# A two-layer encoder: the last layer's second product without a stored S2, with a second pool for weights, and with S1 made in two halves

## Chip, cores and metric

The kernel runs on one core of one Trainium2 chip. The metric is the device time of one execution in microseconds (us), the median of several runs.

## What is computed

The reference is an encoder of two layers over 1024 tokens of 1024 channels, in float32. Each layer has a mixer, a cross attention to 256 memory rows, and a feed-forward part; each of the three is normalised, added to the residual and stored.

```python
for i in range(DEPTH):                      # DEPTH = 2
    h = rms_norm(x, norm_mix[i, 0])
    if i % 2 == 0: mix = pool_and_conv_mixer(h)      # first layer
    else:          mix = s5_and_hyena_mixer(h)       # last layer
    x = x + rms_norm(mix, norm_mix[i, 1])
    h = rms_norm(x, norm_xattn[i, 0])
    m = rms_norm(mem, norm_mem[i])
    x = x + rms_norm(memory_cross_attention(h, m, ...), norm_xattn[i, 1])
    h = rms_norm(x, norm_mlp[i, 0])
    x = x + rms_norm(squared_relu_mlp(h, mlp_w1[i], mlp_w2[i]), norm_mlp[i, 1])

def squared_relu_mlp(xn, w1, w2):           # w1 1024 x 4096, w2 4096 x 1024
    h = jax.nn.relu(xn @ w1)
    return (h * h) @ w2
```

## The kernel before

**Numbers in two parts.** A matrix product is made of three matmuls (`mm3`, L263): each operand is held as a high and a low part in the fp32r format, and high*high, high*low and low*high are summed in PSUM. The two parts come from `split` (L258): a copy on ScalarE (L256) and a subtraction on VectorE (all tensor-tensor operations have L238). A weight block (128 rows by 1024) is therefore loaded as float32 into a buffer, split into a weight tile of twice the size, and used.

**Pools.** SBUF tiles come from pools of a fixed number of buffers: "h" (`hslot`, 9 buffers of 8 KB per partition), "a" (`slot`, 8), "w" (weight tiles, 4), "r" (`raw`, loaded blocks of 512 KB, 2), "t" (`tmp`, 3), "n" (`ntmp`, 3). A pool gives out its buffers in the order in which the program asks for them. In the profile a tile's name starts with its pool's letter, and a label of the stage follows (`wdn`, `adn`, `rdn`: "w", "a" and "r" buffers of the second product).

**Order.** A framework plans the order of the instructions of each engine when the program is built: it goes by due order, and what stands under `tc.high_priority()` goes first, as soon as its buffers are free. Weight loads, splits and the work on PSUM results are marked like that. On an engine the instructions then run strictly in that order; a DMA is issued from the queue of the engine named (`nc.sync`: SyncE, `nc.scalar`: ScalarE, `nc.gpsimd`: GpSimd), and waits there for its buffers.

**The feed-forward parts.** `mlp_up` makes the hidden values by a scheme with seven products in place of eight (sums of blocks in advance). Its loop over p = 0..15 uses `prep(p)` (L736), which loads two weight blocks, forms four sums of them and splits them; `prep(p + 1)` is called ahead of the products of p. In the first layer the loop runs interleaved with the preparation of the S5 mixer (`s5_prep`, L1402, small VectorE operations; it holds one "h" buffer from its start). In the last layer the hidden values are stored in seven forms in a DRAM array `HO`.

**The last layer's second product** is `mlp_q` (L918). It has seven products, i = 0..6, each over eight blocks of the hidden dimension; a step takes two blocks, so there are 28 steps j of 48 matmuls of 512 columns. `a11, a12, a21, a22` are the quarters of w2. Product 2 needs `S2 = S1 - a11`, product 3 `a11 - a21`, product 5 `S1 = a21 + a22`, product 6 `a12 - S2`. `load(j + 1)` is called ahead of step j: it loads two tiles of `HO` through "t" into "h" buffers (`hload`) and two weight blocks (`wload`). Where a block is a difference of two, both are loaded into one "a" buffer, subtracted there and split into a "w" buffer; in product 2 the difference is also stored to the DRAM array `SB` by a DMA on ScalarE's queue (L956), and product 6 loads it again. Four more "a" buffers come to hold the results (U, c11, c12, c22). After product 4 the first half of the tokens gets its residual; the last two steps are run together, token half by token half, and the second half's residual ends the kernel.

**S1** is made by DMAs alone, in `down_sums` (L905): one small DMA that ties its start to a tile `after`, and for each of eight blocks a copy of a21 into the DRAM array `SA` and a DMA that adds a22 to it, all on GpSimd's queue. It is called between the last layer's mixer and its attention. The attention (`attention`, L631) makes the scores (`scores`, L589, with blocks of G as weights), their softmax and the product with VW (`proj_out`, L422, which also does the residual, loading x on GpSimd's queue, L398). The mixer ends in the same `proj_out`, after a gate (`s5_gate`, L1673).

Of the kernel before, what the change touches and what calls it, by code (L numbers as in the profile page):

```python
# [18 lines left out]
P = 128  # L19
# [9 lines left out]
WINDOWS = (2, 4, 8, 16)  # L29
PI = math.pi  # L30
# [155 lines left out]
class Net:  # L186
# [444 lines left out]
    def attention(self, l, GV, H, xsrc, xdst):  # L631
        G, VW = GV
        PT = self.scores(G, H)
        return self.proj_out(VW, lambda hf, k: PT[hf][k], xsrc, self.gain("xattn", l, 1), xdst, self.gain("mlp", l, 0), quads=True)

# [43 lines left out]
    def mlp_up(self, l, B, HID, HO=None):  # L679
# [91 lines left out]
        nxt = prep(0)  # L771
        for p in range(16):
            c, S1, S2, S3, S4, A22 = nxt
            if p < 15:
                nxt = prep(p + 1)
            if HO is not None:
                to = HO[:, p // 2, :, (p % 2) * 512:(p % 2 + 1) * 512].rearrange("i p t -> p i t")
                with self.tc.high_priority():
                    e = self.hslot([4, 512])
                    nc.gpsimd.dma_start(e[:, 0], to[:, 0])  # L780
# [124 lines left out]
    def down_sums(self, l, after):  # L905

        nc = self.nc
        w2 = self.i["mlp_w2q"][l - 1]
        self.S1[l] = S1 = self.dram([8, P, 1024], f"SA{l}")

        nc.gpsimd.dma_start(S1[:, 0, 0:1].rearrange("n c -> c n"), after.bitcast(F32)[0:1, 0:8])
        for n in range(9):
            if n < 8:
                nc.gpsimd.dma_start(S1[n], w2[n, 1, 0])
            if n > 0:
                nc.gpsimd.dma_start(S1[n - 1], w2[n - 1, 1, 1], accum_op=ALU.add, max_dma_last_dim=4096)

    def mlp_q(self, l, B, xsrc, xdst, gnext, res):  # L918
# [10 lines left out]
        S1, S2 = self.S1[l], self.dram([8, P, 1024], f"SB{l}")  # L929
# [3 lines left out]
        s1, s2 = lambda c: S1[c], lambda c: S2[c]  # L933
        prods = [(True, (a11,), 0), (False, (a12,), 1), (True, (s1, a11), 4), (False, (a11, a21), 5),
                 (False, (a22,), 2), (True, (s1,), 3), (False, (a12, s2), 6)]
        steps = [(i, c) for i in range(7) for c in range(0, 8, 2)]

        def hload(i, c):
            t = self.tmp([2, 512])
            nc.gpsimd.dma_start(t[:].rearrange("p a t -> p (a t)"), HO[prods[i][2], c])  # L940
            h = self.hslot([2, 2, 512], F32R)
            self.split(h[:, 0], h[:, 1], t[:])
            return h

        def wload(i, c):
            src = prods[i][1]
            if len(src) == 1:
                return self.wblk(src[0](c))
            r = self.slot([2, 1024])
            for k in range(2):  # L950
                nc.sync.dma_start(r[:, k], src[k](c))
            self.sub(r[:, 0], r[:, 0], r[:, 1])
            w = self.wp.tile([P, 2, 1024], F32R, tag="w", name=self.nm("w"))
            self.split(w[:, 0], w[:, 1], r[:, 0])
            if i == 2:
                nc.scalar.dma_start(S2[c], r[:, 0])  # L956
            return w

        def load(j, h=None):
            i, c = steps[j]  # L960
            with self.tc.high_priority():
                h = h or [hload(i, c + q) for q in range(2)]
                return [wload(i, c + q) for q in range(2)], h
# [9 lines left out]
        for i, _ in enumerate(self.mlp_up(l, B, None, HO)):  # L973
            yield
            if i == 22:
                h = [hload(0, q) for q in range(2)]
# [842 lines left out]
    def mix1(self, H, xsrc, xdst, stop=None):  # L1819
# [70 lines left out]
        rhs = lambda hf, k: tuple(Y[k][:, s, hf * 512:(hf + 1) * 512] for s in range(2))  # L1890
        return self.proj_out(self.i["od_w_out"][0], rhs, xsrc, self.gain("mix", 1, 1), xdst, self.gain("xattn", 1, 0), (4, 5, 6, 7, 0, 1, 2, 3), late=2)

    def run(self, stop=None, first=0):
# [50 lines left out]
        self.down_sums(1, H[1][7][0])  # L1944
# [24 lines left out]
```

## Time and profile before

| what | value |
|---|---|
| median of 3 runs | 2913.18 us (2903.13 to 2919.44) |
| the profiled execution | 2913.07 us, of which the span is 2911.3 us |
| TensorE (PE) busy | 2767.3 us, 95% of the span |
| TensorE weight loads (PEld) busy | 2311.9 us, 79% (beside the matmuls) |
| VectorE (DVE) busy | 2038.3 us, 70% |
| ScalarE (ACT) busy | 1088.0 us, 37% |
| GpSimd (POOL) busy | 260.3 us, 9% |
| moved by DMA | 515.93 MB, mean 177 GB/s |

The page shows one execution; the last columns of a timeline row are the operation, the tiles (output<-inputs), and in brackets the idle time before it with what ended that. Busy shares are means over stages of very different kinds, so a stage is read by itself: the first layer's `mlp_up` lies at about 711 to 1048 us, the last layer's mixer ends at about 2050 (its output product starts near 1925), its scores lie at about 2048 to 2165, the attention's output product follows until about 2250, `mlp_up` until 2576, and the second product until the end. TensorE's matmuls are pipelined, so a busy TensorE need not be at its full pace; the number of matmuls in a stretch tells the pace.

### The profile page before, as it was taken

How to read it: one execution, taken by the hardware profiler on the slowest of the kernel's cores; microseconds unless marked ns; L12 is line 12 of the kernel's file. 1: busy time of each engine (PE TensorE's matmuls, PEld its weight loads, DVE VectorE, ACT ScalarE, POOL GpSimd, SP SyncE). 2: the span in 40 equal slices, each digit the busy share in tenths (PEclk: the TensorE clock that was granted, in tenths of full speed). 3: DMA queues.
4: the chain of work that ended last, by engine and by line, in shares of the span. 5: the costliest groups of instructions: out<-in, count | busy, mean ns of one | idle time of the engine just before them, and what ended most of it. 6: DMA issues, size and time to landing. Idle time of an engine off the chain costs nothing. (4 is left out here: it accounts for less than half of the span.)

```text
span 2911.3 us, 35912 instructions
## 1 busy us (share of the span) xinstructions
PE 2767.3 (95%) x13832; PEld 2311.9 (79%) x13832; DVE 2038.3 (70%) x3375; ACT 1088.0 (37%) x1304; POOL 260.3 (9%) x468
## 2 busy tenths in 40 slices
PE   8998999999999999999999988889999999998997
PEld 7877888988777877788878877768988778777886
DVE  6676546847899756695877788955846878755676
ACT  4344324444543442222343211233433544453341
POOL 0000000000211111010000000000010222210010
PEclk9999999999999999999999999999999999999999
DMA  5582214324644464342347688744363766688672
GB/s 177 209 286 102 69 44 138 102 87 145 230 170 145 143 199 137 121 152 80 120 161 234 218 264 272 276 160 129 114 185 119 241 227 224 216 282 319 225 262 104
DMA packets 177011, 515.93 MB, mean 177 GB/s; under 512 B 18820, under 2 KB 64008, under 8 KB 169672
## 3 DMA queue, kind: packets, MB, share of 16 engines
q1 hardware_dynamic: 87160, 244.99, 25.6%
q0 software_dynamic: 57872, 238.06, 23.7%
q10 hardware_dynamic: 31808, 30.60, 3.1%
q8 instruction: 108, 1.77, 0.2%
q14 instruction: 63, 0.52, 0.1%
HBM read 380.40 MB, written 141.56 MB: 179 GB/s over the span
## 5 line engine op out<-in xcount | busy, mean ns | idle before, releaser
L265 PE MATMUL mdn<-hdn,wdn 128*128 128x512 f32 (+1 forms) x752 | 287.4, 382 | 7.8 <-ACT wdn L256 7.5
L266 PE MATMUL mdn<-hdn,wdn 128*128 128x512 f32 (+1 forms) x752 | 287.4, 382 | 0.0
L267 PE MATMUL mdn<-hdn,wdn 128*128 128x512 f32 (+1 forms) x752 | 287.2, 382 | 0.0
L265 PEld LDWEIGHTS mdn<-hdn,wdn 128*128 128x128 f32 x752 | 142.0, 189 | 36.3 <-ACT wdn L256 8.3
L265 PE MATMUL mup<-apre,wup 128*128 128x512 f32 x384 | 153.4, 399 | 13.6 <-DVE hup L238 13.5
L266 PEld LDWEIGHTS mdn<-hdn,wdn 128*128 128x128 f32 x752 | 142.0, 189 | 27.5 <-issue 0.6
L267 PEld LDWEIGHTS mdn<-hdn,wdn 128*128 128x128 f32 x752 | 142.0, 189 | 27.4 <-DVE wdn L238 1.0
L267 PE MATMUL mup<-apre,wup 128*128 128x512 f32 x384 | 151.7, 395 | 0.1
L266 PE MATMUL mup<-apre,wup 128*128 128x512 f32 x384 | 151.8, 395 | 0.0
L256 ACT ACTIVATE wup<-rup 128x1024 fp32r<-128x1024 f32 x69 | 73.0, 1060 | 194.8 <-PE mup L267 183.0
L265 PE MATMUL msc<-wsc,hpre 128*128 128x256 f32 x448 | 128.3, 286 | 1.6 <-ACT hpre L256 1.6
L266 PE MATMUL msc<-wsc,hpre 128*128 128x256 f32 x448 | 129.5, 289 | 0.0
L267 PE MATMUL msc<-wsc,hpre 128*128 128x256 f32 x448 | 128.5, 288 | 0.4 <-DVE hpre L238 0.4
L238 DVE TENSOR_TENSOR hup<-hup,mup 128x512 f32<-128x512 f32 x128 | 87.5, 684 | 57.5 <-PE mup L267 56.4
L238 DVE TENSOR_TENSOR hdn<-tdn,hdn 128x1024 fp32r<-128x1024 f32 x74 | 90.4, 1222 | 52.3 <-ACT hdn L256 52.0
L266 PE MATMUL mmx<-hpre,wmx 128*128 128x512 f32 x320 | 124.7, 390 | 0.0
L256 ACT ACTIVATE hdn<-tdn 128x1024 fp32r<-128x1024 f32 x74 | 78.2, 1056 | 124.6 <-PE mdn L267 100.3
L265 PE MATMUL mmx<-hpre,wmx 128*128 128x512 f32 x320 | 124.7, 390 | 0.0
L267 PE MATMUL mmx<-hpre,wmx 128*128 128x512 f32 x320 | 124.5, 389 | 0.0
L238 DVE TENSOR_TENSOR wout<-rout,wout 128x1024 fp32r<-128x1024 f32 x48 | 58.7, 1222 | 87.6 <-ACT wout L256 87.6
L256 ACT ACTIVATE wdn<-rdn 128x1024 fp32r<-128x1024 f32 x53 | 55.9, 1056 | 140.7 <-PE mdn L267 129.4
L265 PE MATMUL mue<-hpre,wue 128*128 128x512 f32 x256 | 101.1, 395 | 1.1 <-ACT tue L256 1.1
(520 smaller groups left out, 7848.3 us busy)
## 6 DMA issues: line engine op xcount, KB each, us to landing
tdn<-HO POOLq DMA_DIRECT2D x50, 512.0 KB, 4.9
nres<-x POOLq DMA_DIRECT2D x44, 512.0 KB, 5.0
rup<-mlp_w SPq DMA_DIRECT2D x33, 512.0 KB, 3.9
x<-hout POOLq DMA_DIRECT2D x32, 512.0 KB, 5.1
rue<-mlp_w SPq DMA_DIRECT2D x32, 512.0 KB, 3.8
hup<-mlp_w SPq DMA_DIRECT2D x32, 512.0 KB, 4.4
wmx<-fwd POOLq DMA_DIRECT2D x16, 1024.0 KB, 7.3
HO<-hup POOLq DMA_DIRECT2D x16, 1024.0 KB, 6.0
```

Source lines behind the costliest of these rows:

```text
L238: self.nc.vector.tensor_tensor(out=out, in0=a, in1=b, op=op)
L256: self.nc.scalar.activation(out, a, AF.Copy)
L265: t.matmul(out, l[0], r[0], start=start, stop=False, **kw)
L266: t.matmul(out, l[0], r[1], start=False, stop=False, **kw)
L267: t.matmul(out, l[1], r[0], start=False, stop=stop, **kw)
```

## The change

It has four parts. (1) Product 2's difference is no longer stored: `SB` and its eight stores are gone, and product 6 makes its weights from three loaded operands, `a12 + S1 - a11`. (2) Loaded operands go elsewhere: where there are two or three, the first two go into one "h" buffer and a third into an "r" buffer; the split weights of every odd step go into an "a" buffer, those of even steps into a "w" buffer as before; within a load all fetches come first, then the weights' splits, then those of `HO`. (3) `down_sums` makes four blocks of S1 per call: the first four are tied to the gate's last output and called ahead of the mixer's `proj_out`, the other four are tied to the last head of the second token half and called between the scores and the attention's `proj_out`. (4) In the first layer's `mlp_up`, `prep(p)` is called at the start of iteration p; in the last layer nothing changes there.

```diff
--- before.py
+++ after.py
@@ -27,6 +27,7 @@
 MAGIC = 12582912.0
 RSQ = float(0x5F3759DF)
 WINDOWS = (2, 4, 8, 16)
+QUADS = (1,)
 PI = math.pi
 
 
@@ -631,6 +632,8 @@
     def attention(self, l, GV, H, xsrc, xdst):
         G, VW = GV
         PT = self.scores(G, H)
+        if l in QUADS:
+            self.down_sums(l, 1, PT[1][0][0])
         return self.proj_out(VW, lambda hf, k: PT[hf][k], xsrc, self.gain("xattn", l, 1), xdst, self.gain("mlp", l, 0), quads=True)
 
 
@@ -768,12 +771,11 @@
                 nc.gpsimd.dma_start(c[:, 0], P1[p])
             return c, S1, S2, S3, S4, (w[:, 0], w[:, 1])
 
-        nxt = prep(0)
+        nxt = prep(0) if HO is not None else None
         for p in range(16):
-            c, S1, S2, S3, S4, A22 = nxt
-            if p < 15:
-                nxt = prep(p + 1)
+            c, S1, S2, S3, S4, A22 = nxt or prep(p)
             if HO is not None:
+                nxt = prep(p + 1) if p < 15 else None
                 to = HO[:, p // 2, :, (p % 2) * 512:(p % 2 + 1) * 512].rearrange("i p t -> p i t")
                 with self.tc.high_priority():
                     e = self.hslot([4, 512])
@@ -902,17 +904,20 @@
             with self.tc.high_priority(offset=300 if hf == 0 else 0):
                 res.append(finish(hf, acc))
 
-    def down_sums(self, l, after):
+    def down_sums(self, l, part, after):
 
         nc = self.nc
         w2 = self.i["mlp_w2q"][l - 1]
-        self.S1[l] = S1 = self.dram([8, P, 1024], f"SA{l}")
-
-        nc.gpsimd.dma_start(S1[:, 0, 0:1].rearrange("n c -> c n"), after.bitcast(F32)[0:1, 0:8])
-        for n in range(9):
-            if n < 8:
+        if part == 0:
+            self.S1[l] = self.dram([8, P, 1024], f"SA{l}")
+        S1 = self.S1[l]
+        lo = 4 * part
+
+        nc.gpsimd.dma_start(S1[lo:lo + 4, 0, 0:1].rearrange("n c -> c n"), after.bitcast(F32)[0:1, 0:4])
+        for n in range(lo, lo + 5):
+            if n < lo + 4:
                 nc.gpsimd.dma_start(S1[n], w2[n, 1, 0])
-            if n > 0:
+            if n > lo:
                 nc.gpsimd.dma_start(S1[n - 1], w2[n - 1, 1, 1], accum_op=ALU.add, max_dma_last_dim=4096)
 
     def mlp_q(self, l, B, xsrc, xdst, gnext, res):
@@ -926,41 +931,52 @@
         nc = self.nc
         w2 = self.i["mlp_w2q"][l - 1]
         HO = self.dram([7, 8, P, 1024], f"HO{l}")
-        S1, S2 = self.S1[l], self.dram([8, P, 1024], f"SB{l}")
+        S1 = self.S1[l]
 
 
         a11, a12, a21, a22 = [lambda c, m=m, q=q: w2[c, m, q] for m in range(2) for q in range(2)]
-        s1, s2 = lambda c: S1[c], lambda c: S2[c]
+        s1 = lambda c: S1[c]
         prods = [(True, (a11,), 0), (False, (a12,), 1), (True, (s1, a11), 4), (False, (a11, a21), 5),
-                 (False, (a22,), 2), (True, (s1,), 3), (False, (a12, s2), 6)]
+                 (False, (a22,), 2), (True, (s1,), 3), (False, (a12, s1, a11), 6)]
         steps = [(i, c) for i in range(7) for c in range(0, 8, 2)]
 
-        def hload(i, c):
+        def hfetch(i, c):
             t = self.tmp([2, 512])
             nc.gpsimd.dma_start(t[:].rearrange("p a t -> p (a t)"), HO[prods[i][2], c])
+            return t
+
+        def hparts(t):
             h = self.hslot([2, 2, 512], F32R)
             self.split(h[:, 0], h[:, 1], t[:])
             return h
 
-        def wload(i, c):
+        def wfetch(i, c):
             src = prods[i][1]
-            if len(src) == 1:
-                return self.wblk(src[0](c))
-            r = self.slot([2, 1024])
-            for k in range(2):
-                nc.sync.dma_start(r[:, k], src[k](c))
-            self.sub(r[:, 0], r[:, 0], r[:, 1])
-            w = self.wp.tile([P, 2, 1024], F32R, tag="w", name=self.nm("w"))
-            self.split(w[:, 0], w[:, 1], r[:, 0])
-            if i == 2:
-                nc.scalar.dma_start(S2[c], r[:, 0])
+            rs = []
+            if len(src) > 1:
+                r = self.hslot([2, 1024])
+                rs += [r[:, 0], r[:, 1]]
+            if len(src) != 2:
+                rs.append(self.raw.tile([P, 1024], F32, tag="r", name=self.nm("r"))[:])
+            for r, x in zip(rs, src):
+                nc.sync.dma_start(r, x(c))
+            return rs
+
+        def wparts(rs, odd):
+            for x, op in zip(rs[1:], (ALU.subtract, ALU.add)):
+                self.tt(rs[0], rs[0], x, op)
+            w = self.slot([2, 1024], F32R) if odd else self.wp.tile([P, 2, 1024], F32R, tag="w", name=self.nm("w"))
+            self.split(w[:, 0], w[:, 1], rs[0])
             return w
 
-        def load(j, h=None):
+        def load(j, hs=None):
             i, c = steps[j]
+            cs = range(c, c + 2)
             with self.tc.high_priority():
-                h = h or [hload(i, c + q) for q in range(2)]
-                return [wload(i, c + q) for q in range(2)], h
+                rs = [wfetch(i, c) for c in cs]
+                ts = hs or [hfetch(i, c) for c in cs]
+                ws = [wparts(r, j % 2) for r in rs]
+                return ws, hs or [hparts(t) for t in ts]
 
         def run(t, ws, hs, i, first, stop, tok=slice(0, 512)):
             for q, (w, h) in enumerate(zip(ws, hs)):
@@ -973,7 +989,7 @@
         for i, _ in enumerate(self.mlp_up(l, B, None, HO)):
             yield
             if i == 22:
-                h = [hload(0, q) for q in range(2)]
+                h = [hparts(hfetch(0, q)) for q in range(2)]
         nxt = load(0, h)
         acc = None
         for j, (i, c) in enumerate(steps):
@@ -1888,6 +1904,7 @@
         merge((self.s5_gate(*gg, Y), 8), (gv, 3))
         Y += hy
         rhs = lambda hf, k: tuple(Y[k][:, s, hf * 512:(hf + 1) * 512] for s in range(2))
+        self.down_sums(1, 0, Y[3][:, 0])
         return self.proj_out(self.i["od_w_out"][0], rhs, xsrc, self.gain("mix", 1, 1), xdst, self.gain("xattn", 1, 0), (4, 5, 6, 7, 0, 1, 2, 3), late=2)
 
     def run(self, stop=None, first=0):
@@ -1941,7 +1958,6 @@
         if stop == "mix1":
             return
         x2 = dst("x5", "att1")
-        self.down_sums(1, H[1][7][0])
         H = self.attention(1, self.GV[1], H, x1, x2)
         if stop == "att1":
             return
```

## Rows read from the trace of the kernel before

**Rows 1.** The page: busy us (share of the span) and instructions.

```profile
PE 2767.3 (95%) x13832; PEld 2311.9 (79%) x13832; DVE 2038.3 (70%) x3375; ACT 1088.0 (37%) x1304; POOL 260.3 (9%) x468
```

**Rows 2.** Table of stages: window, length, engines' busy us (instructions), clock, DMA share, GB/s.

```profile
2650.00:2675.00 25.00, 25.00 (x112) 20.71 (x111) 13.43 (x12) 9.95 (x10) 2.29 (x5) 1.00 0.96 348
2675.00:2700.00 25.00, 17.42 (x66) 13.39 (x65) 13.01 (x11) 6.97 (x7) 1.59 (x3) 0.80 0.88 324
```

**Rows 3.** Waits of TensorE, 2600 to 2860: us in total, times, longest us.

```profile
PE mdn L265 <- ACT wdn L256: 7.5, 1, 7.5
PE mdn L265 <- DVE adn L238: 0.3, 1, 0.3
```

**Rows 4.** Timelines of SP, DVE, ACT, PE, 2650 to 2695 [idle before].

```profile
2653.24 0.32 SPq L951 DMA_DIRECT2D adn<-SA  x1
2666.02 24.35 SPq L951 DMA_DIRECT2D adn<-mlp_w2q  x10
...
2677.03 1.23 DVE L238 TENSOR_TENSOR adn<-adn 128x1024 f32<-128x1024 f32 x1 [2.06 <-DMA adn<-mlp_w2q]
...
2678.29 3.04 ACTq L956 DMA_DIRECT2D SB<-adn  x2
2683.34 1.06 ACT L256 ACTIVATE wdn<-adn 128x1024 fp32r<-128x1024 f32 x1 [5.34 <-DMA SB<-adn]
...
2684.45 0.79 PE L265 MATMUL mdn<-hdn,wdn 128*128 128x512 f32 x1 [7.54 <-ACT wdn L256]
```

**Rows 5.** DMA, 2640 to 2700: 40 slices, total, issues (us to landing).

```profile
GB/s 339 235 161 371 382 388 401 423 415 415 423 404 407 388 169 303 322 279 164 360 385 279 391 418 415 426 412 339 314 246 350 134 270 401 347 350 320 82 322 396
DMA packets 5486, 20.02 MB, mean 334 GB/s; under 512 B 607, under 2 KB 607, under 8 KB 5482
...
adn<-mlp_w2q SPq DMA_DIRECT2D x15, 512.0 KB, 7.8
...
SB<-adn ACTq DMA_DIRECT2D x6, 512.0 KB, 5.0
```

**Rows 6.** Table of stages and chain (start, us, what) in the scores.

```profile
2110.00:2120.00 10.00, 10.00 (x85) 10.00 (x84) 3.51 (x4) 2.12 (x2) 3.57 (x5) 1.00 0.98 260
...
2130.00:2140.00 10.00, 6.58 (x45) 6.39 (x44) 4.29 (x10) 4.08 (x11) 2.12 (x3) 0.84 1.02 297
...
2120.01 11.27 DMA rsc<-G
...
2136.55 1.67 PE xsc L626 x8
```

**Rows 7.** Timeline of GpSimd's queue, 1900 to 2310.

```profile
1999.34 0.53 POOL L398 DMA_DIRECT2D nres<-x  x1 [78.75 <-DVE nout L238]
...
2105.42 0.53 POOL L911 DMA_DIRECT2D SA<-hpre  x1 [34.83 <-ACT hpre L256]
...
2143.03 0.83 POOL L916 DMA_DIRECT2D SA<-mlp_w2q  x1 [4.10 <-DMA SA<-mlp_w2q]
2206.24 0.58 POOL L398 DMA_DIRECT2D nres<-x  x1 [62.38 <-issue]
```

**Rows 8.** Table of stages; DVE near 1956; DMA issues 2165 to 2200.

```profile
1950.00:1975.00 25.00, 25.00 (x112) 20.69 (x111) 6.96 (x8) 8.29 (x11) 0.00 (x0) 1.00 0.18 61
...
1955.94 0.69 DVE L238 TENSOR_TENSOR amx<-tmx,amx 128x512 fp32r<-128x512 f32 x1 [0.70 <-ACT amx L256]
...
rout<-VW SPq DMA_DIRECT2D x4, 512.0 KB, 3.1
```

**Rows 9.** Table of stages, at the start of product 5.

```profile
2800.00:2825.00 25.00, 24.85 (x113) 20.09 (x112) 22.95 (x36) 10.52 (x11) 5.29 (x10) 1.00 0.69 239
```

**Rows 10.** DMA, 2800 to 2870: total.

```profile
DMA packets 4042, 15.80 MB, mean 226 GB/s; under 512 B 452, under 2 KB 452, under 8 KB 3782
```

**Rows 11.** Waits of TensorE, 700 to 1060 and then 2254 to 2580.

```profile
PE mup L265 <- DVE hup L238: 10.6, 7, 2.5
...
PE mup L265 <- DVE hup L238: 7.0, 5, 2.9
```

## The prediction

> **What bounds the kernel now.** I read the page's line of engines first: TensorE is busy 95% of the span [rows 1]. So the question for each part of the change is only whether TensorE stands still less, or more. The table of stages gives the pace: a stretch in which TensorE is never short of work has 112 matmuls of 512 columns in 25 us, 0.223 us each, with DVE and ACT about half idle beside them [rows 2]. Where a stretch of the same kind has fewer, the missing count times 0.223 us is the loss, and it contains both the standstill and the slower matmuls behind it. In the last layer's second product (from 2576 us to the end) one stretch falls short, 2675 to 2700, with 66 [rows 2]; in that layer's attention another does, 2130 to 2140, where 45 matmuls of 256 columns stand beside 85 in an undisturbed ten microseconds [rows 6]. The list of TensorE's waits from 2600 to 2860 holds nothing but 7.5 us in the first of these places and one wait of 0.3 us [rows 3]. These two places are what the change can reach; the first layer's loop order touches a third.
>
> **Part 1: the S2 store goes.** The S2 stores are eight DMAs on ScalarE's queue, L956. The timelines of 2650 to 2690 show what they do [rows 4]. SyncE's queue issues a load at 2653.24 and the next only at 2666.02: it waits for one of the eight "a" buffers, which a store still reads (a store lands 5.0 us after its issue [rows 5]). The loads that then go out together take 7.8 us by their median [rows 5]; DVE's subtraction waits for one until 2677.03; ScalarE has two stores in its queue at 2678.29, behind subtractions; and the split of the weights that TensorE needs comes behind both, at 2683.34. TensorE stood for 7.54 us until 2684.45 [rows 4], and the clock granted in the stretch is 0.80 [rows 2]: part of what follows ran at the lower of the two levels, 1.2 of 2.4 GHz. In all 112 - 66 = 46 matmuls are missing: 46 x 0.223 = **10.3 us**. All three links (the buffer held by a store, the stores ahead of a split on ScalarE, the bytes of the store among the loads) are gone in the new code. The DMA work of a step of the third product falls from 8 blocks of 512 KB (four operands, two of HO, two stores) to 6, which is 3.15 MB in a step of 48 x 0.223 = 10.7 us, 294 GB/s; the mean from 2640 to 2700 was 334 GB/s [rows 5]. What is late next there is the load of the third product's first operands: pairs now need "h" buffers, of which nine serve four tiles of HO in use and prepared, and the pairs, so a pair is asked for about one and a half steps, 16 us, ahead. A load of 7.8 us and some 3.6 us of subtracting and splitting (three operations like the 1.23 us of [rows 4]) fit into that. I take the whole 10.3 us; the bounds are 0 (a stall of the same size in its place) and 10.3.
>
> **Part 2: other buffers for odd steps.** Weights of odd steps leave the "w" pool (four buffers) for the "a" pool (eight, of which four will hold results). That makes room for two more steps of prepared weights. It takes no instruction off any engine, and TensorE has no other wait in these steps [rows 3], so by itself it is worth nothing; it is the cover for parts 1 and 4. The order inside a load also changes (weights ahead of HO); HO is asked for ahead of its use too, so I cost that at nothing. Without that cover it would be one load, the 7.8 us of [rows 5].
>
> **Part 3: S1 in two halves.** Now all 17 DMAs of S1 are issued on GpSimd's queue from 2105 to 2143 [rows 7], in the middle of the scores, where the DMA share is 0.98 to 1.02 [rows 6]. The chain shows a load of G beside them from 2120.01 over 11.27 us, then the split of its weights on ScalarE, behind that split the exponentials, and the transposes of these, for which TensorE waited, from 2136.55 [rows 6]; a load of the same size later takes 3.1 us [rows 8]. Missing: 85 - 45 = 40 matmuls at 10/85 = 0.118 us, 4.7 us. With the DMAs gone the split is early and the exponentials follow; a border of the softmax can still leave a few tenths, so I take **4.5 us** (bounds 0 and 4.7). What the halves cost where they go: the issues of eight blocks span 38 us here, so four take some 20 and a landing. The first half may start when the gate's last output is there (1956 [rows 8]) and is over by about 1980; the DMA share is 0.18 there, TensorE runs at its full 112 [rows 8], and GpSimd's queue has nothing until 1999.34 [rows 7]. The second follows the last transposes of the scores, and GpSimd's queue is idle from 2143 to 2206 [rows 7]. In both stretches weights are being loaded, one block of 512 KB for 24 matmuls, 5.4 us, with two raw blocks ahead, so a load that takes 11.3 instead of 3.1 us is still there in time. Both cost nothing; if that cover failed once, it would be the same 4.7 us again. The waits between a block's copy and its addition stay on GpSimd's queue; behind them only the loads of the residual's x are queued, at 1999 and 2206.
>
> **Part 4: the seventh product's weights.** They are made from three operands, a12 + S1 - a11, instead of two: eight more loads of 512 KB and eight more DVE additions of 1.23 us [rows 4], 10 us of DVE in all over four steps, beside a stretch where DVE is busy 22.95 of 25 us at its worst [rows 9]; no earlier than that do they begin, and TensorE has prepared weights then, so DVE hides them. The DMAs are the tighter side. A step of the seventh product asks for 8 blocks in 10.7 us, 4.19 MB or 392 GB/s, as the third product did with its stores, and the residual of the first half and its output move nearby too. From 2800 to 2870 the old kernel moved 15.8 MB [rows 10]. The change adds 8 blocks, and I estimate another 8 (half of the S2 loads with their partners) that were fetched earlier into "a" buffers and can now come only later: 24.2 MB until 2868, when the last weights are wanted, 356 GB/s. That is more than the mean of 334 and less than the fortieths with 401 to 426 GB/s [rows 5]. With two steps of weights prepared ahead I take nothing; the bounds are 0 and the 33 us of the second rival. The Trainium skill (HBM Reference, Specifications (TRN2)) speaks against this part: it gives a core an effective 358 GB/s. By that alone a step of 4.19 MB would take 11.7 us as an estimate, four steps would end 4 us late, and the sum would be 2902; the fortieths above 400 GB/s differ from it, so the measurement decides.
>
> **Part 5: the first layer's loop.** The weights of iteration p are asked for in iteration p instead of one earlier. Both are marked to go first, and buffers of a pool are given out in the program's order, which for the buffers of this loop stays the same; only the side work (the S5 preparation) asks for its one "h" buffer one iteration sooner, before the second iteration's. No instruction is added. TensorE waits there for DVE additions that queue behind preparation work, 10.6 us in 7 waits, and the same loop in the last layer, without side work, has 7.0 in 5 [rows 11]. A new order can shorten or lengthen these: bounds -10.6 and +10.6, taken as 0, since the same work stays on the same engines.
>
> **The sum.** The profiled execution took 2913.07 us, its span being 2911.3; the median of the three runs is 2913.18, so it stands for them (they spread from 2903 to 2919). 2913.1 - 10.3 - 4.5 = 2898.3, so **2898**.
>
> **The rivals.** *The tail gets short of DMA in part.* At 334 GB/s the 24.2 MB take 72.5 us, the last weights come 4 to 5 us late, and the lower clock behind a standstill costs 2 to 3 more (of the 10.3 us above 7.54 were standstill): 2905. For it: the 392 GB/s of a step; against it: the old tail has 0.3 us of waiting [rows 3] and the new one has more weights prepared. *The tail gets short altogether, slower than before.* If the queues carry only the 239 GB/s of 2800 to 2825 [rows 9], 24.2 MB take 101 us, 33 us late: 2931. It ends above the old time from 291 GB/s downward (83 us, 15 late). Against it: those 239 were what was asked for, with a DMA share of 0.69. *The first layer gains:* its seven waits vanish, 2898 - 10.6 = 2887. *The first layer loses:* they double, 2909. *The stall of part 1 stays,* because a pair of operands in "h" buffers comes as late as one in an "a" buffer did: 2908; against it, the store's landing is what freed the buffer.
>
> **How the numbers follow.** Forecast 2898, by itself 2892 to 2904, 0.50. Tail short in part (2905) 0.14; short altogether (2931) 0.10; first layer gains (2887) 0.11; first layer loses (2909) 0.08; the stall stays (2908) 0.07. A measurement of this kernel tells some 0.5%, 14.6 us, from no change, so the borders are 2898.6 and 2927.7, and the forecast lies just under the first. Of its half I put 0.33 below the border and 0.17 above. Faster is 0.33 and the first layer's 0.11, 0.44; slower is the 0.06 of the slow tail that lies above 2927.7, with 0.01 of a first layer that loses more, 0.07; same is the rest, 0.49. The range from 2886 to 2915 leaves out the slow tail and the ends of the first layer's cases.
>
> **What would show it.** Part 1: 112 matmuls in each 25 us from 2600 on, no wait of TensorE over 1 us there, no fall of the clock. Part 3: no short stretch in the second half of the scores, G loads near 3 us, S1 at about 1956 to 1980 and behind the scores, with full counts beside both. Part 4: the last four steps at full pace, or else waits for splits of the seventh product's weights with DMA shares near 1. Part 5: the seven waits between 700 and 1060. The prediction is wrong if a wait of several microseconds stands in the third or the seventh product, or if the stretches before 1900 move by more than 5 us.

## The result, and the profile after

| | before | after |
|---|---|---|
| median, run beside each other | 2916.31 us | 2883.65 us (2880.91 to 2891.65) |
| profiled execution | 2913.07 us | 2882.18 us, span 2880.4 us |

The ratio is 0.9899 [0.9858, 0.9939]: 29.5 us less by the ratio (41 to 18 by the interval, 32.7 by the medians) where 15 were forecast. The direction was right; the time lies 14 us under the forecast and 2.4 us under the range's lower end.

The page of after: TensorE works 9 us less than in [rows 1] and the span is 30.9 us shorter, so 22 us of the gain are standstill and the rest is faster running.

```profile
PE 2758.3 (96%) x13832; PEld 2307.0 (80%) x13832; DVE 2046.5 (71%) x3383; ACT 1089.9 (38%) x1304; POOL 261.0 (9%) x469
```

The table of stages of after (columns as in [rows 2]). The first two rows answer [rows 2], the third is the seventh product, the fourth is in the scores [rows 6], the last three are where S1 is made now.

```profile
2650.00:2675.00 25.00, 25.00 (x112) 20.72 (x111) 14.10 (x12) 7.92 (x8) 2.65 (x5) 1.00 0.82 292
2675.00:2700.00 25.00, 25.00 (x112) 20.71 (x111) 21.84 (x19) 12.06 (x12) 2.12 (x4) 1.00 0.68 244
...
2800.00:2825.00 25.00, 23.21 (x102) 18.54 (x101) 21.54 (x21) 8.98 (x10) 2.13 (x4) 1.00 0.96 353
...
2120.00:2130.00 10.00, 9.85 (x83) 9.57 (x83) 4.89 (x9) 4.05 (x10) 0.00 (x0) 1.00 0.33 107
...
1925.00:1950.00 25.00, 25.00 (x112) 20.72 (x111) 10.96 (x15) 8.60 (x14) 5.86 (x9) 1.00 0.69 189
1950.00:1975.00 25.00, 25.00 (x112) 20.70 (x111) 7.26 (x6) 9.77 (x10) 0.00 (x0) 1.00 0.40 107
...
2150.00:2175.00 25.00, 25.00 (x112) 20.70 (x111) 6.03 (x5) 7.02 (x8) 3.88 (x5) 1.00 0.80 210
```

TensorE's waits of after, from 2600 to 2860 (answering [rows 3]) and then the longest group from 700 to 1060 [rows 11]:

```profile
PE mdn L266 <- DVE adn L239: 1.8, 2, 0.9
...
PE mup L266 <- DVE hup L239: 5.9, 5, 1.7
```

The 7.5 us at 2684 are gone, both stretches around S1's new places run at the full 112, and the first layer's waits fell from 10.6 to 5.9 us, in a part to which the forecast gave nothing. Counted on TensorE's records: the first layer's second product begins to use weights of its own stage 13.5 us earlier (1044.7 for 1058.2), of which 10.2 are left at its end (1422.4 for 1432.6); the scores' last block ends 21.6 earlier (2135.7 for 2157.3), the kernel ends 30.9 earlier. Some 2 of the first two figures lie ahead of the first layer's `mlp_up`, where nothing was changed, which leaves about 8 for the loop at that end.

### The profile page after: what moved, and what is told of

The parts are those of the page before. It is cut to its first block, busy times and chain, and to the rows that moved or that the text cites. A ratio compares the mean times of both kernels' runs of the same rounds, so it can differ in the third digit from the quotient of the medians.

```text
span 2880.4 us, 35930 instructions
## 1 busy us (share of the span) xinstructions
PE 2758.3 (96%) x13832; PEld 2307.0 (80%) x13832; DVE 2046.5 (71%) x3383; ACT 1089.9 (38%) x1304; POOL 261.0 (9%) x469
## 5 line engine op out<-in xcount | busy, mean ns | idle before, releaser
L266 PE MATMUL mdn<-hdn,wdn 128*128 128x512 f32 (+1 forms) x544 | 208.7, 384 | 1.8 <-DVE adn L239 1.8
L267 PE MATMUL mdn<-hdn,wdn 128*128 128x512 f32 (+1 forms) x544 | 208.9, 384 | 0.0
L268 PE MATMUL mdn<-hdn,wdn 128*128 128x512 f32 (+1 forms) x544 | 208.8, 384 | 0.0
L266 PEld LDWEIGHTS mdn<-hdn,wdn 128*128 128x128 f32 x544 | 102.3, 188 | 22.6 <-issue 1.4
L267 PEld LDWEIGHTS mdn<-hdn,wdn 128*128 128x128 f32 x544 | 102.3, 188 | 20.4 <-issue 0.6
L268 PEld LDWEIGHTS mdn<-hdn,wdn 128*128 128x128 f32 x544 | 102.3, 188 | 19.6
L239 DVE TENSOR_TENSOR aup<-aup,mdn 128x1024 f32<-128x1024 f32 x56 | 68.1, 1216 | 49.5 <-PE mdn L268 49.3
```

The costliest lines, as they stand in the source:

```text
L239: self.nc.vector.tensor_tensor(out=out, in0=a, in1=b, op=op)
L266: t.matmul(out, l[0], r[0], start=start, stop=False, **kw)
L267: t.matmul(out, l[0], r[1], start=False, stop=False, **kw)
L268: t.matmul(out, l[1], r[0], start=False, stop=stop, **kw)
```

## Experiments: the three parts alone

The change falls into three independent pieces: the loop order, the halves of S1, and the new second product (`mlp_q`). Each was put alone into the kernel before; a fourth kernel is the changed one without the loop order.

**The loop order alone.**

```diff
-        nxt = prep(0)
+        nxt = prep(0) if HO is not None else None
...
-            c, S1, S2, S3, S4, A22 = nxt
-            if p < 15:
-                nxt = prep(p + 1)
+            c, S1, S2, S3, S4, A22 = nxt or prep(p)
             if HO is not None:
+                nxt = prep(p + 1) if p < 15 else None
```

> The kernel before with the first layer's loop order alone. By the comparison of the two traces the first layer's loop ends 11 us earlier in the changed kernel, and 10 us of that are still there when its second product ends. If the loop order is the cause, this kernel is 8 to 12 us faster than before (ratio 0.996 to 0.997) and its span from 700 to 1060 us has the fuller stretches of the changed kernel. Rival: the first layer's gain came with a new plan of all instructions, whichever part of the change brought it; then this one is within 3 us of before.

2905.99 us, ratio 0.9973 [0.9963, 0.9984]: 7.9 us less, at the edge of what the loop's case gave and not the rival's 3 or less.

**The halves of S1 alone** (`down_sums` with its `part`, its two calls, and the old ones gone).

> The kernel before with S1 made in two halves alone. The scores lost 4.7 us beside S1's DMAs, and the traces show 7 us between the mixer's output product and the attention's. If S1's place is the cause, 5 to 7 us faster, and no short stretch in the second half of the scores. Rival: the halves cost in their new places what they free in the scores; then within 2 us of before.

2907.46 us, 0.9977 [0.9966, 0.9988]: 6.7 us less.

**The new second product alone** (no store of S2, three operands in the seventh product, the new buffers and the new order in a load).

> The kernel before with the second product's part alone: no S2 store, three operands in the seventh product, operands in h and r buffers, odd weights in a buffers. If the stall at 2677 us goes and nothing takes its place, 10 to 11 us faster. Rival: the seventh product's third operand gets the tail short of DMA: 5 us or less.

2900.29 us, 0.9948 [0.9932, 0.9965]: 15.2 us less; the 10 to 11 of its case lie at the low end of the interval.

**The changed kernel with the old loop order.**

> The changed kernel with the first layer's weights asked for one iteration ahead again. If the loop order brought the first layer's gain, this is 8 to 12 us slower than the changed kernel, so 18 to 21 us faster than before. Rival (a new plan brought it): no more than 3 us slower than the changed kernel, about 27 us faster than before.

2893.17 us, 0.9932 [0.9914, 0.9951]: 19.8 us less than before, 9.5 more than the changed kernel.

Gains are worked out from the ratios; a comparison of two changed kernels is of their medians. The three parts add up: 7.9 + 6.7 + 15.2 = 29.8, measured 29.5. Within their intervals, 3 to 5 us either way, nothing is lost or gained between them, so each can be looked into by itself. The old loop order costs 7.9 us in one kernel and 9.5 in the other.

## Experiments: the first layer's loop

The trace of before names two places that are gone after. First the table of stages, then TensorE's waits at 817, 1030 and 1049 and, between the last two, ScalarE and VectorE ahead of the second:

```profile
800.00:825.00 25.00, 21.95 (x92) 16.98 (x93) 19.06 (x38) 9.80 (x12) 3.34 (x7) 1.00 0.53 182
1025.00:1050.00 25.00, 20.05 (x84) 15.80 (x83) 13.99 (x17) 12.27 (x14) 3.73 (x7) 0.93 0.53 168
...
816.72 0.50 PE L265 MATMUL xup<-apre,wup 128*128 128x512 f32 x1 [1.70 <-ACT wup L256]
...
1030.29 0.50 PE L265 MATMUL mup<-apre,wup 128*128 128x512 f32 x1 [2.48 <-DVE hup L238]
...
1025.51 1.06 ACT L256 ACTIVATE hup<-tup 128x1024 fp32r<-128x1024 f32 x1 [4.94 <-DMA tup<-HID]
1026.61 1.23 DVE L238 TENSOR_TENSOR hup<-tup,hup 128x1024 fp32r<-128x1024 f32 x1 [5.77 <-ACT hup L256]
1028.35 0.68 DVE L238 TENSOR_TENSOR hup<-hup,mup 128x512 f32<-128x512 f32 x1
1029.55 0.68 DVE L238 TENSOR_TENSOR hup<-hup,mup 128x512 f32<-128x512 f32 x1
...
1048.81 0.50 PE L265 MATMUL mup<-apre,wup 128*128 128x512 f32 x1 [2.48 <-DVE hup L238]
```

VectorE stood 5.77 us at a split of hidden values (`hup<-tup`, the first load for the second product), which waited for ScalarE's half of it, which waited 4.94 us for the load from `HID`. The two additions that set TensorE free come behind it. In the new loop order that load is traced ahead of the last `prep`, not behind it, and so gets its "t" and "h" buffers sooner. At 817 the split of a weight is late instead.

**The load alone**: the first load of hidden blocks one step earlier in the kernel before.

```diff
         for i, _ in enumerate(up):
             yield
-            if i == 22:
+            if i == 21:
                 nxt = [load(0, 0)]
```

> The kernel before with one change in the first layer: the first load of hidden blocks for the second product is traced one step earlier, ahead of the last preparation, as the restored loop order also has it. Theory A (the late load's splits stand ahead of TensorE's sums on VectorE at 1027 and 1047, 28 matmuls missing in that 25 us): the two waits of 2.48 us go and with the slow pace behind them 5 to 6 us in all, ratio 0.998. Theory B (the gain of the loop order lies in the preparations of every step, not in this load): within 1.5 us of before.

2908.50 us, 0.9981 [0.9966, 0.9997]: 5.5 us less.

**The first step alone**: the new order for p = 0, the old one from p = 1 on.

```diff
-        nxt = prep(0)
+        nxt = prep(0) if HO is not None else None
...
-            c, S1, S2, S3, S4, A22 = nxt
-            if p < 15:
-                nxt = prep(p + 1)
+            c, S1, S2, S3, S4, A22 = nxt or prep(p)
+            nxt = prep(p + 1) if p < 15 and (HO is not None or p > 0) else None
```

> The kernel before with the first layer's loop order restored for its first step alone: the second step is prepared after the first one's products, and from there on each step ahead as before. Theory A (the first step's weights stand on ScalarE behind a split that waits for a transfer, 1.7 and 0.5 us at 817, 19 matmuls missing there): 2 to 4 us faster than before, ratio 0.999. Theory B (all of the gain is the load of hidden blocks at the end of the loop, or every step's preparation): within 1 us of before.

2913.25 us, 0.9988 [0.9972, 1.0004]: 3.5 us less, with 0 just inside the interval. The tables of stages of the two, the load's kernel first:

```profile
800.00:825.00 25.00, 21.44 (x91) 16.46 (x90) 18.39 (x39) 9.18 (x11) 4.33 (x9) 1.00 0.53 181
1025.00:1050.00 25.00, 25.00 (x113) 20.05 (x112) 20.24 (x32) 14.68 (x17) 3.70 (x7) 1.00 0.70 235
```

```profile
800.00:825.00 25.00, 23.89 (x105) 19.37 (x104) 21.12 (x34) 13.09 (x15) 4.87 (x10) 1.00 0.76 264
1025.00:1050.00 25.00, 19.70 (x73) 15.65 (x73) 14.94 (x19) 10.88 (x13) 3.73 (x7) 0.82 0.55 181
```

Each kernel mends its own place and not the other: the load fills 1025 to 1050 (113 matmuls for 84) and not 800 to 825; the first step does the reverse (105 for 92). The same holds over all the kernels: from 800 to 825 there are 86 to 98 matmuls with the old first step and 105 to 112 with the new one, from 1025 to 1050 there are 72 to 97 with the old load and 113 or 114 with the early one. So theory A held in both places. In time this is weaker: the 3.5 us of the first step are not told from nothing, and in its profiled execution the 73 matmuls for 84 at the second place, within the spread of the old load, take most of the gain back. The sum 5.5 + 3.5 = 9.0 stands beside 7.9 and 9.5 for the whole and needs no share of "every step's preparation", but it does not shut a small one out.

## Experiments: the second product

Here the forecast had named one cause, the store. The whole part gave 15.2 us; these kernels take it apart. The first and the last three are the changed kernel with something undone; the second and the third are the kernel before with something done.

**The store kept** in the changed kernel.

```diff
-                  (False, (a22,), 2), (True, (s1,), 3), (False, (a12, s1, a11), 6)]
+                  (False, (a22,), 2), (True, (s1,), 3), (False, (a12, s2), 6)]
...
+            if keep is not None:
+                nc.scalar.dma_start(keep, rs[0])
```

> The changed kernel with the store of S2 put back: the second of the seven products stores its sum S2 on ScalarE's queue, and the seventh reads a12 and S2 instead of a12, S1 and a11; the alternating pools of the weights stay. Theory A (the store alone costs the 7.5 us stall at 2684 and what follows it): ten or more microseconds come back, 2893 to 2899, 0.993 to 0.995 of the kernel before. Theory B (the pools bring it: with more room for weights the store holds nothing up): 2882 to 2887, 0.989 to 0.991. About half each (2889) would mean that the stall falls to both.

2888.05 us (2886.10 to 2889.31), 0.9908 [0.9885, 0.9931]: 4.4 us above the changed kernel by the medians and 2.6 by the ratios, with runs of both in the same band. The ratio lies in theory B's range, the time between theory B and the case of half each.

**The store taken out** of the kernel before, its buffers and order kept.

> The kernel before, without the store of S2 and with the seventh product from a12, S1 and a11, but with every weight of the second product in the one pool as before. Alone with the alternating pools this part gave 15.2 us. Theory A (store alone): 2899 to 2903, 11 to 15 us faster than before. Theory B (pools alone): 2911 to 2916, at most 3 us faster. If it is 5 to 10 us faster, both have a share, the rest of the 15.2 being the pools'.

2911.54 us, 0.9985 [0.9968, 1.0002]: 4.4 us less (3.5 by the medians), not told from nothing. Theory A is out here. With the store kept it is out as well, but for the last bit of the interval: theory A began at 0.993, the interval ends at 0.9931.

**The same with the weights ahead of the hidden blocks** in each load.

> The kernel before without the store of S2, with every weight in the one pool and the pairs where they were, but with each load's weights fetched and split ahead of its hidden blocks, as in the changed kernel. Without that order it took 2911.5, 3.5 us less than before, with a wait of 4.6 us at 2687. Theory B (the order): the wait goes, 2900 to 2904. Theory A (room) or C (pairs in h buffers): 2909 to 2914, the wait stays at 4 us or more.

2914.43 us, 1.0001 [0.9985, 1.0018]. The order by itself brings nothing; the wait of 4.6 us stayed.

**The weights of all steps in one pool**, in the changed kernel.

```diff
-            w = self.slot([2, 1024], F32R) if odd else self.wp.tile([P, 2, 1024], F32R, tag="w", name=self.nm("w"))
+            w = self.wp.tile([P, 2, 1024], F32R, tag="w", name=self.nm("w"))
```

> The changed kernel, with one thing undone: the weights of odd steps go into the pool of four that the even ones use; the pairs of operands stay in h buffers, the weights are still split ahead of the hidden blocks, S2 is not stored. The kernel before without the store but with its old pools and order was only 3.5 us faster than before, so some 11 of the second product's 15 us lie in the pools or in the order of a load. Theory A (the room for two more steps of weights): 2893 to 2897, 10 us and more above the changed kernel, ratio near 0.993 to 0.995. Theory B (the order, weights ahead of hidden blocks on ScalarE and VectorE) or C (the pairs in h buffers): 2883 to 2887, ratio 0.989 to 0.991.

2895.63 us (2892.85 to 2899.80), 0.9942 [0.9928, 0.9956]: 12.0 us above the changed kernel (12.5 by the ratios), as theory A had it.

**The hidden blocks ahead of the weights**, in the changed kernel.

> The changed kernel, with one other thing undone: in each load the hidden blocks are fetched and split ahead of the weights, as before; the alternating pools, the pairs in h buffers and the missing store stay. Theory A (room for weights): the same as the changed kernel, 2882 to 2887, ratio 0.989 to 0.991. Theory B (the order: before, splits of hidden blocks that wait for TensorE to free an h buffer stood ahead of the weights' splits on ScalarE): 2890 to 2896, ratio 0.992 to 0.995.

2886.53 us (2880.39 to 2895.72), 0.9906 [0.9888, 0.9923]: not told from the changed kernel. Its runs spread over 15 us, though, and in the profiled one, the longest, 23 matmuls are missing from 2675 to 2700.

**The store kept and one pool**, both.

> The changed kernel with two things undone: the weights of odd steps go into the pool of four, and the second product stores S2, which the seventh reads with a12. What stays of the second product's part is the pairs in h buffers and the order in a load. Undone alone, the store gave back some 3 to 4 us (2888) and the pool some 12 (2895.6). Theory A (two separate costs): 2898 to 2901, ratio 0.995 to 0.996. Theory B (one cause: the store does harm only where weights have no room, and the stall of 10.3 us at 2684 is the store's under that condition): 2902 to 2908, ratio 0.9965 to 0.998. Theory C (without room the weights are late anyway, and the store adds nothing): 2894 to 2897, ratio near 0.994.

2891.04 us (2889.92 to 2894.93), 0.9925 [0.9906, 0.9945]: none of the three numbers. Next to one pool alone, the store with its two operands is 4.6 us faster (the intervals just overlap), where next to the changed kernel it was 4.4 us slower: the prices of these edits depend on each other.

The stretch that holds the stall of before, 2675 to 2700, in the tables of stages of four of them: store taken out of before; store kept; one pool; store kept and one pool (the last two with a later stretch).

```profile
2675.00:2700.00 25.00, 20.33 (x79) 15.86 (x78) 16.33 (x14) 8.02 (x8) 2.12 (x4) 0.86 0.69 250
```

```profile
2675.00:2700.00 25.00, 24.70 (x108) 19.94 (x108) 18.02 (x16) 8.80 (x10) 2.12 (x4) 1.00 0.81 297
```

```profile
2675.00:2700.00 25.00, 21.67 (x83) 17.34 (x83) 16.91 (x16) 8.48 (x10) 2.12 (x4) 0.86 0.66 253
...
2825.00:2850.00 25.00, 22.42 (x91) 17.85 (x91) 22.62 (x21) 10.64 (x13) 1.59 (x3) 0.93 0.96 371
```

```profile
2675.00:2700.00 25.00, 21.79 (x95) 17.42 (x94) 16.38 (x16) 8.23 (x9) 2.12 (x4) 1.00 0.72 269
...
2825.00:2850.00 25.00, 24.27 (x113) 20.00 (x112) 17.97 (x18) 12.25 (x14) 0.55 (x2) 1.00 0.53 198
```

Of 112 matmuls 46 are missing before [rows 2]; 33 without the store; with the pairs in h buffers and one pool, 29 without the store and 17 with it; with two pools, 4 with the store and none without. Taking the store out leaves most of the stall standing; all the new buffers together remove nearly all of it with the store in place.

But these counts mix two stalls, because the kernels come to 2675 at different points of their work. TensorE's waits from 2600 to 2860 tell them apart: store taken out of before; one pool; store kept and one pool.

```profile
PE mdn L265 <- ACT wdn L256: 4.6, 1, 4.6
```

```profile
PE mdn L266 <- DVE adn L239: 5.9, 2, 3.3
```

```profile
PE mdn L266 <- DVE adn L239: 3.9, 3, 2.6
```

The stall of before is a wait for the split of a weight (`wdn`). It comes behind 441 matmuls of the second product, counted from the end of `mlp_up`, in before and in all six of its variants that keep the pairs of operands in "a" buffers, with or without the store, with either order of a load. The seven kernels with the pairs in "h" buffers do not have it, not even with the store kept and one pool. So the place of the pairs decides on it. With one pool another stall follows, 120 matmuls later, on the sum of a finished product (`adn`); the second pool removes that one. It is there once with two pools, in the long execution with hidden blocks first.

No kernel moves the pairs alone. As an estimate, with some 6 us either way, the move and the new order of a load gave 7.2 us where the store and one pool stayed (21.8 by the ratio of the last kernel, less the 7.9 and 6.7 of loop and S1), and 2.3 with one pool and no store (16.9 less the same): the later stall takes much of the gain back.

What is late when the store is gone, in the kernel before without it (SyncE's queue and VectorE; then TensorE, ScalarE, VectorE):

```profile
2658.25 0.32 SPq L951 DMA_DIRECT2D adn<-SA  x1
2670.04 18.55 SPq L951 DMA_DIRECT2D adn<-mlp_w2q  x7
...
2668.79 1.22 DVE L238 TENSOR_TENSOR wdn<-adn,wdn 128x1024 fp32r<-128x1024 f32 x1
...
2686.56 0.79 PE L265 MATMUL mdn<-hdn,wdn 128*128 128x512 f32 x1 [4.63 <-ACT wdn L256]
...
2681.97 1.06 ACT L256 ACTIVATE hdn<-tdn 128x1024 fp32r<-128x1024 f32 x1 [4.38 <-PE mdn L267]
2683.05 1.22 DVE L238 TENSOR_TENSOR hdn<-tdn,hdn 128x1024 fp32r<-128x1024 f32 x1 [0.81 <-ACT hdn L256]
2684.20 1.22 DVE L238 TENSOR_TENSOR adn<-adn 128x1024 f32<-128x1024 f32 x1
...
2685.45 3.90 ACT L256 ACTIVATE wdn<-adn 128x1024 fp32r<-128x1024 f32 x4 [2.43 <-DVE adn L238]
```

SyncE's queue stands for 11.8 us between two loads, for 12.8 with the store [rows 4]. Here the second load goes out as VectorE ends a weight's split, at 2670.0: the split holds the "a" buffer, and the store had held it only about 1 us longer. Four weights are split in one go at 2685.45, as late as with the store (2683.34, [rows 4]): the subtraction ahead of them stands behind the split of a hidden block, for which ScalarE waited on TensorE. And the later stall, with one pool in the changed kernel (ScalarE twice, VectorE, TensorE):

```profile
2664.82 1.07 ACT L257 ACTIVATE wdn<-hdn 128x1024 fp32r<-128x1024 f32 x1 [5.57 <-PE mdn L268]
...
2685.59 1.06 ACT L257 ACTIVATE hdn<-tdn 128x1024 fp32r<-128x1024 f32 x1 [8.25 <-DVE wdn L239]
...
2691.23 1.21 DVE L239 TENSOR_TENSOR adn<-adn,mdn 128x1024 f32<-128x1024 f32 x1
...
2692.59 0.77 PE L266 MATMUL mdn<-hdn,wdn 128*128 128x512 f32 x1 [3.33 <-DVE adn L239]
```

With four weight buffers a weight can be split only when TensorE gives one back (5.57 us of waiting at 2664.82). All the preparation behind it bunches up, and VectorE's addition of a finished sum (`adn<-adn,mdn`), which gives TensorE its PSUM tile back, stands behind the bunch. The wait has another name in each kernel (a weight, a sum, a store); the shortage behind it is one of buffers, of the "a" pool for the first stall and of the "w" pool for the second.

The number of weight pools goes with the start of the second product too: in the end of the last layer's `mlp_up` TensorE's longest wait is 2.6 to 3.1 us in eight of the nine kernels with one pool (1.8 in the ninth) and 0.6 to 1.6 us in all five with two. From 2550 to 2600 that is 193 matmuls before and 209 with the product alone: 16 x 0.223 = 3.6 us that the forecast did not have.

## Why the prediction was right and wrong

**Part 1, the store, -10.3: place right, cause wrong.** The 46 missing matmuls came back, but the step that failed is "All three links [...] are gone in the new code" and with it "I take the whole 10.3 us". It took the store for what held up the chain. Without the store SyncE still waits 11.8 us for its "a" buffer and 33 matmuls are missing; the store's own share is some 3 to 4 us in either kernel (by the ratios 4.4 in the old and 2.6 in the new, by the medians 3.5 and 4.4), and neither is told from nothing. What removed the stall is the move of the pairs, which the part named only as a new condition ("pairs now need "h" buffers"). That the term came out near its size is luck: the change held the true remedy beside the supposed one.

**Part 2, other buffers, 0: a cover, as forecast, and more.** "TensorE has no other wait in these steps [rows 3], so by itself it is worth nothing": the list of waits could not show the stall on sums that comes when the first one is gone and the weights have one pool. As a cover the room was priced at one load, 7.8 us; measured it is 12.0 by the medians (12.5 by the ratios), and 3.0 (5.0 by the ratios) with the store kept. The sum of parts 1 and 2 came out at 15.2 [10.2 to 19.8] where 10.3 stood, and the start of the product, which part 2 had at nothing, is 3.6 of the difference.

**Part 3, S1, -4.5: mechanism right, size too small.** 6.7 [3.5 to 9.9]. The stretch at 2130 is at its full pace, S1's halves run beside full stretches, and no cover failed. GpSimd's queue in after, answering [rows 7], shows when each half begins and issues its last DMA:

```profile
1929.50 0.53 POOL L916 DMA_DIRECT2D SA<-amx  x1 [23.71 <-ACT amx L257]
...
1948.98 0.81 POOL L921 DMA_DIRECT2D SA<-mlp_w2q  x1 [9.45 <-DMA SA<-mlp_w2q]
...
2143.99 0.52 POOL L916 DMA_DIRECT2D SA<-asc  x1 [89.12 <-ACT asc L257]
...
2165.46 0.83 POOL L921 DMA_DIRECT2D SA<-mlp_w2q  x1 [9.92 <-DMA SA<-mlp_w2q]
```

The first half starts sooner than the 1956 I had read: that is about 1942 here, 13.5 us being gained before. The DMA that ties it reads four elements of the gate's output, and it goes out behind a split on ScalarE, not behind the last addition on VectorE that I had taken for it. What the sum left out is an early part of the scores. In the 20 us behind the last matmul on the weights that were prepared ahead of the scores (2059.6 in before, 2046.6 in after) TensorE does 134 to 145 matmuls in the seven kernels with S1 in its old place, and 164 to 166 in the seven with the halves; before and after:

```profile
2059.60:2079.60 20.00, 17.62 (x145) 17.45 (x144) 15.55 (x25) 8.26 (x8) 2.66 (x5) 0.98 0.72 237
```

```profile
2046.60:2066.60 20.00, 19.95 (x166) 19.70 (x165) 18.13 (x31) 8.68 (x10) 1.60 (x3) 1.00 0.65 232
```

At 0.118 us each, 21 matmuls are 2.5 us, and 4.5 + 2.5 = 7.0 stands beside the 6.7. The place in before (GpSimd's queue, VectorE, TensorE), and the same load and addition in after:

```profile
2060.40 0.54 POOL L404 DMA_DIRECT2D x<-hout  x1 [4.87 <-DVE hout L238]
2060.93 0.53 POOL L398 DMA_DIRECT2D nres<-x  x1
...
2068.54 1.23 DVE L238 TENSOR_TENSOR hout<-hout,nres 128x1024 f32<-128x1024 f32 x1 [2.76 <-DMA nres<-x]
...
2076.51 1.02 PE L317 MATMUL xpre<-ones,npre 128*128 128x1 f32 x8 [2.38 <-DVE npre L238]
```

```profile
2045.26 0.54 POOL L405 DMA_DIRECT2D x<-hout  x1 [2.71 <-DVE hout L239]
2045.78 0.53 POOL L399 DMA_DIRECT2D nres<-x  x1
...
2052.83 1.23 DVE L239 TENSOR_TENSOR hout<-hout,nres 128x1024 f32<-128x1024 f32 x1
```

The last load of the residual's x is issued 1.3 us behind 2059.6 in before and 0.8 ahead of 2046.6 in after; VectorE no longer waits for it. In both it stands in GpSimd's queue behind a store that waits for VectorE, 4.87 us in before and 2.71 in after. S1 was not running there in either kernel, so this is the order of work on the queues, not its traffic. Why moving S1 moves that load was not settled.

**Part 4, the third operand, 0: right within 2 us.** From 2800 to 2825 the changed kernel has 102 of 112 matmuls, 2.2 us lost; with the store kept, that is with two operands, it has 104 there. The DMA work is heavy, as feared, 0.96 of the DMA time at 353 GB/s, but TensorE's two waits there, of 0.9 us at most, are for finished sums on VectorE. That the cover is the room of part 2 is what the one-pool kernel suggests: with three operands its last steps fall to 91 matmuls at a clock of 0.93, with two they have 113. Operands and store change together there, so which of them does it is argued, not shown; and the kernel before without the store, with three operands and one pool but the old buffers and order, has the full 112 at the same place of its work (2845 to 2870) and no wait over 0.2 us in its last steps. The rivals "short in part" and "short altogether" did not come. The figure that spoke against this part was misread: the effective 358 GB/s for a core is the share of a core while both cores of a pair are streaming, and the Trainium skill (HBM Reference, Specifications (TRN2)) puts a core that streams alone well above it; this kernel runs on one core. The kernel with the new product alone shows more over a whole stretch:

```profile
2825.00:2850.00 25.00, 23.47 (x103) 18.83 (x102) 23.56 (x23) 10.68 (x12) 1.60 (x3) 1.00 1.01 383
```

383 GB/s over 25 us, so as a border for a step that figure does not hold here. The Trainium skill (Perfetto Trace Analysis, Roofline) puts a lone core's ceiling near 435 GB/s; the trace is near it, 435 being the highest of the 40 slices of 1.75 us from 2775 to 2845 of after, and 445 where the slices are cut from 2800 on:

```profile
GB/s 393 323 360 300 363 328 279 255 342 288 281 265 307 419 424 414 424 162 337 267 360 421 372 311 407 337 344 360 405 405 433 435 403 103 0 0 0 0 0 0
```

**Part 5, the loop, 0: wrong.** The bounds (10.6 either way) held it: 7.9 alone, 9.5 in the changed kernel. The step that failed is "buffers of a pool are given out in the program's order, which for the buffers of this loop stays the same". It looked at the loop and not at what is traced between two of its iterations: the first load of the second product changes places with the last `prep`, and takes its "t" and "h" buffers first. The rival "the first layer gains" (2887, 0.11) had the right side, though not by its seven waits vanishing: five stay, with 5.9 us. By the prediction's own sign, stretches before 1900 that move by more than 5 us, it is wrong here: they moved by up to 13.5.

**The sum.** 2913.1 - 15.2 - 6.7 - 7.9 = 2883.3, beside 2883.65; with intervals of 3 to 5 us on each term, so close a fit is in part chance. The forecast was short by 4.9 in parts 1 and 2, 2.2 in part 3 and 7.9 in part 5, 15.0 in all. All three erred the same way; the only case that reached below 2892, a gain in the first layer, had 0.11.

## What to carry over

The releaser at the end of a chain is the last of several that may be late together: before a stall is put down to it, ask when the next one would have come, and take away the one suspect alone on the chip. When a stall stays in the same stretch after such a change, ask whether it is still at the same instruction; here two stalls shared one window. In a pipeline that prepares its operands ahead, count the buffers between the stages first; too few of them show as waits with a new name each time (a store, a split, a sum not added in time). Moving the pairs to another pool removed what taking out the store did not, and a second pool for the weights kept the next wait from taking its place. When a call is moved in a program whose buffers are given out in its order, list what else is traced between the old place and the new.

## What the runs showed of the hardware

Two things were not expected. The lower clock makes much of a short wait: in the kernel with the first step alone, waits of 3.26 and 2.04 us between 1025 and 1050 left 73 matmuls of the 114 that the new order has there, 41 x 0.22 = 9 us, at a granted clock of 0.82 in that stretch, while with the store and one pool a wait of 2.57 us and one of 0.64 left 95 of 112 at 1.00. And one core alone moved 383 GB/s over 25 us with the DMA engines' share at 1.01, while TensorE did 103 of its 112 matmuls.
